# One load tile in four pieces beside the first store, and GpSimdE in charge of the critical section

## Chip, cores and metric

The kernel runs on one core of a Trainium2 chip. The metric is the time of one execution on the device in microseconds. Several chips of the same kind were used. Kernels submitted together ran on one chip, together with new runs of the kernel before, so every comparison has its own yardstick.

## The reference

A softmax over groups of 544 values. The whole tensor is read once and written once, 285 MB each way.

```python
B, N, D, G = 4, 4096, 4352, 8
x_g = x.reshape(B, N, G, D // G)
exp = np.exp(x_g - x_g.max(axis=-1, keepdims=True))
out = (exp / exp.sum(axis=-1, keepdims=True)).reshape(B, N, D)
```

## The kernel before

The 16,384 rows are cut into 64 tiles of 128 partitions with two rows each: 34,816 bytes per partition, 4.456 MB per tile. Six buffers are used in turn. Each tile is loaded, reduced to its maxima (VectorE), exponentiated with sums (ScalarE), multiplied in place by the reciprocal sums (VectorE) and stored. Loads are issued by SyncE, stores by GpSimdE except the last two. The load of tile t waits until the store of tile t-6 has landed on all 16 DMA engines.

```python
ctx.enter_context(tc.tile_critical(no_gpsimd_drain=True))
bufs = [... nc.sbuf_tensor(f"xt{b}", [P, R * D], f32) ... for b in range(NT)]   # NT = 6
...
for t in range(nt):                                   # SyncE: loads, nt = 64
    if t >= NT:
        nc.sync.wait_ge(stored[t % NT], 16 * (t // NT))
    tile_in = bufs[t % NT]
    if t < nt - 1:
        nc.sync.dma_start(out=tile_in[:, :], in_=xt[t]).then_inc(landed[t % NT], 16)
    else:
        ...                                           # the last tile in two halves
for t in range(nt - LAST, nt):                        # SyncE: the last two stores
    nc.sync.wait_ge(scaled, t + 1 if t < nt - 1 else len(parts))
    nc.sync.dma_start(out=ot[t], in_=bufs[t % NT][:, :]).then_inc(last_stored, 16)
nc.sync.wait_ge(last_stored, 16 * LAST)

for t in range(nt - LAST):                            # GpSimdE: the other stores
    nc.gpsimd.wait_ge(scaled, t + 1)
    nc.gpsimd.dma_start(out=ot[t], in_=bufs[t % NT][:, :]).then_inc(stored[t % NT], 16)
...
```

## Time and profile before

| | kernel before |
|---|---|
| time, median of the first 3 runs | 1326.64 us (1326.55 to 1326.76) |
| span in the profile | 1324.9 us |
| rate of the 16 DMA engines, 300 to 1200 us | 433 GB/s |
| time per tile in the middle, load to load | 20.61 us |
| VectorE busy | 1190.0 us, 90% |

The DMA engines are the bound; the prediction shows the lines. In profile lines VectorE is DVE, ScalarE ACT, GpSimdE POOL and SyncE SP; the DMA queue q0 (software_dynamic) carries GpSimdE's stores, q1 (hardware_dynamic) what SyncE issues. Besides the page, the trace holds every DMA packet (queue, size, start, duration) and, for each transfer, 16 landings, one per DMA engine. In a load the distance of the 16th landing from the first tells how far the slowest engine is behind.

### The profile page before, as it was taken

Reading aid. Unit: us, or ns where it says so; the run is one execution under the profiler, and the core shown is the slowest. Engines: PE = TensorE matmul, PEld = TensorE weight load, DVE = VectorE, ACT = ScalarE, POOL = GpSimd, SP = SyncE. Lnnn points to the kernel's source line nnn. Section 1 sums busy time; section 2 is a strip of 40 time slices with the busy share of each in tenths; the row PEclk is TensorE's granted clock in tenths of the full one; section 3 lists DMA queues with packets and bytes.
Section 4 is the critical chain, followed back from the end, with each engine's and each line's share of the span. In section 5 each row is a group of like instructions: output and inputs, shape, how many; then the busy total and the mean of one; then the engine's idle time right before and its main releaser. Section 6 shows DMA issues by size and latency. Waiting matters only on the chain.

```text
span 1324.9 us, 2463 instructions
## 1 busy us (share of the span) xinstructions
DVE 1190.0 (90%) x195; ACT 757.5 (57%) x2049; POOL 33.4 (3%) x66
## 2 busy tenths in 40 slices
DVE  5999999988989889898898998988989889898893
ACT  3765566547456465564655646556465474654751
POOL 0000000000000000000000000000000000000000
DMA  9999999999999999999999999999999999999998
GB/s 404 421 432 436 428 435 434 434 431 433 433 435 433 432 434 433 436 429 435 432 436 431 433 433 434 434 431 435 433 436 429 435 432 436 431 432 434 433 431 372
DMA packets 18582, 570.48 MB, mean 431 GB/s; under 512 B 2064, under 2 KB 2064, under 8 KB 2064
## 3 DMA queue, kind: packets, MB, share of 16 engines
q1 hardware_dynamic: 9648, 294.13, 51.5%
q0 software_dynamic: 8928, 276.30, 48.3%
q14 instruction: 6, 0.05, 0.0%
HBM read 285.21 MB, written 285.21 MB: 431 GB/s over the span
## 4 chain that ended last, share of the span: by engine, by line
another core or an unknown queue 69%; DVE 20%; DMA 7%; ACT 1%; SPq 1%; issue 0%
DVE xt L74 10%; DVE mx L61 10%; DMA out_dram<-xt 4%; DMA xt<-in_x_dram 4%; ACT xt L85 1%; SPq L104 1%; DVE rs L71 0%; SPq L166 0%; SPq L47 0%
## 5 line engine op out<-in xcount | busy, mean ns | idle before, releaser
L85 ACT ACTIVATE xt<-xt,mx 128x544 f32<-128x544 f32 x1024 | 750.2, 734 | 542.7 <-DVE mx L61 542.7
L61 DVE TENSOR_REDUCE mx<-xt 128x16 f32<-128x8704 f32 (+1 forms) x65 | 590.1, 9079 | 111.0 <-DMA xt<-in_x_dram 111.0
L74 DVE TENSOR_TENSOR xt<-xt,rs 128x8704 f32<-128x8704 f32 (+1 forms) x65 | 590.6, 9086 | 2.2
L85 ACT ACTIVATION_READ_ACCUMULATOR xt<-xt,mx 128x1 f32 x1024 | 191.8, 187 | 0.0
L118 POOL DMA_DIRECT2D out_dram<-xt x62 | 33.2, 535 | 1243.7 <-DVE xt L74 1243.7
L71 DVE RECIPROCAL rs<-sm 128x16 f32<-128x16 f32 (+1 forms) x65 | 15.7, 242 | 2.8 <-ACT xt L85 2.8
L123 ACT ACT_TABLE_LOAD x1 | 1.3, 1283 | 0.9 <-SPq L47 0.9
L155 POOL MEMSET const-float32-0.0<- 128x1 f32 x1 | 0.1, 99 | 0.2 <-issue 0.2
L155 POOL MEMSET const-bfloat16-1.0<- 128x1 bf16 x1 | 0.1, 102 | 0.0
L155 POOL MEMSET const-float32-1.0<- 128x1 f32 x1 | 0.1, 99 | 0.0
L155 POOL MEMSET const-uint8-127<- 128x1 uint8 x1 | 0.1, 99 | 0.0
## 6 DMA issues: line engine op xcount, KB each, us to landing
xt<-in_x_dram SPq DMA_DIRECT2D x63, 4352.0 KB, 33.1
out_dram<-xt POOLq DMA_DIRECT2D x62, 4352.0 KB, 50.6
out_dram<-xt SPq DMA_DIRECT2D x2, 4352.0 KB, 20.1
xt<-in_x_dram SPq DMA_DIRECT2D x2, 2176.0 KB, 36.0
```

The source lines that it names most:

```text
L61: i = nc.vector.reduce_max(out=mx[:, t % NT, g], in_=groups(t, g), axis=X, negate=True)
L71: nc.vector.reciprocal(out=rs[:, t % NT, g], in_=sm[:, t % NT, g]).wait_op(exp_done, n + 1, "sem-ge").then_inc(rec_done, 1)
L74: nc.vector.tensor_tensor(out=xg, in0=xg, in1=rs[:, t % NT, g].unsqueeze(2).to_broadcast([P, g.stop - g.start, Dg]), op=mybir.AluOpType.mu ...
L85: i = nc.scalar.activation(out=xg[:, g - gs.start, :], in_=xg[:, g - gs.start, :], func=Exp, bias=mx[:, t % NT, g:g + 1], scale=1.0, accum ...
L104: nc.sync.dma_start(out=tile_in[:, :], in_=xt[t]).then_inc(landed[t % NT], 16)
L118: nc.gpsimd.dma_start(out=ot[t], in_=bufs[t % NT][:, :]).then_inc(stored[t % NT], 16)
L123: nc.scalar.preload_act_table(Exp)
L155: nc = _bacc.Bacc("TRN2", target_bir_lowering=False, num_devices=1)
```

## The change

The intent: when the first store joins the running loads, about one microsecond of DMA time is lost, and the tile then being loaded is tile 4. Its packets are cut to a quarter of their length (8.7 KB). Also, GpSimdE signals the start and the end of the critical section (the `tile_critical` block, in which the kernel orders its engines by its own semaphores) in place of SyncE, to save a hop.

```diff
+    FINE, PIECES = 4, 4
...
-    ctx.enter_context(tc.tile_critical(no_gpsimd_drain=True))
+    ctx.enter_context(tc.tile_critical(
+        sync_engine=mybir.EngineType.Pool, no_gpsimd_drain=True))
...
-            i.wait_op(landed[t % NT], 16 * (t // NT + 1), "sem-ge")
+            more = PIECES - 1 if t % NT == FINE else 0
+            i.wait_op(landed[t % NT], 16 * (t // NT + 1 + more), "sem-ge")
...
-        if t < nt - 1:
+        if t == FINE:
+            for k in range(PIECES):
+                c = slice(k * R * D // PIECES, (k + 1) * R * D // PIECES)
+                nc.sync.dma_start(out=tile_in[:, c], in_=xt[t, :, c]).then_inc(landed[t], 16)
+        elif t < nt - 1:
...
-    nc.sync.wait_ge(last_stored, 16 * LAST)
...
     nc.gpsimd.drain()
+    nc.gpsimd.wait_ge(last_stored, 16 * LAST)
```

## The prediction

> **What bounds the kernel now.** I read the page's slices first, then busy time by stretches, then the DMA view of single stretches, last the instructions at the end. In the slices the 16 DMA engines read 9 or more all the way:
>
> ```profile
> DVE  5999999988989889898898998988989889898893
> DMA  9999999999999999999999999999999999999998
> GB/s 404 421 432 436 428 435 434 434 431 433 433 435 433 432 434 433 436 429 435 432 436 431 433 433 434 434 431 435 433 436 429 435 432 436 431 432 434 433 431 372
> HBM read 285.21 MB, written 285.21 MB: 431 GB/s over the span
> ```
>
> VectorE looks almost as full, but its row dips to 8 in most slices while the DMA row never does. The same in stretches (columns: us, VectorE, ScalarE and GpSimdE busy, clock, DMA share, GB/s):
>
> ```profile
> 0.00:5.00 5.00, 0.00 (x0) 1.28 (x1) 0.20 (x4) 1.00 0.69 223
> 300.00:1200.00 900.00, 811.97 (x131) 518.36 (x1405) 23.45 (x44) 1.00 1.00 433
> 1318.00:1321.00 3.00, 0.00 (x0) 0.00 (x0) 0.00 (x0) 1.00 0.62 267
> 1321.00:1324.90 3.90, 0.00 (x0) 0.00 (x0) 0.00 (x0) 1.00 0.02 9
> ```
>
> So the kernel is bound by 570.4 MB at 433.3 GB/s, 1316.5 us of the 1324.9 us span. I added up the trace's packets in order of time to see where the other 8.4 us go. About 3.0 us are lost in the first 5 us, until loads flow. About 0.9 us are lost between 46 and 51 us and nowhere else in the middle: in single microseconds the rate is 425, 401, 292, 280 and 378 GB/s, then 433 again. The rest is the end: 15 of the 16 engines finish the last store between 1320.3 and 1322.0 us, one at 1323.53 us, and 1.37 us of closing follow. That one engine falls behind all through the run: its part of a load lands 0.24 us after the median part for tile 0, 0.98 us at 308 us, 2.93 us for the last load. It sets the end, so what counts is the time saved on it.
>
> The hole at 46 to 51 us is the one place that the first part of the change touches. The first store is issued at 44.88 us, its first packets start at 49.9 us, and meanwhile load packets that always take 1288 ns are stretched, the longest to 2801 ns. The extra time of those packets sums to 0.90 us per engine. Tile 4 is indeed the tile then in flight: tile 3 lands at 45.2 us and tile 4 at 62.5 us.
>
> **What the Trainium skill says.** The page "DMA: Bandwidth & Descriptors", section "Queues, rings and completion order", says that each DMA engine goes round the queues that have work, one packet each. The trace agrees. With 34.8 KB packets on both sides loads and stores get half each, but in 1263 to 1269 us, where the last tile's loads have 17.4 KB packets, the shares are 2 to 1:
>
> ```profile
> q0 software_dynamic: 51, 1.74, 67.1%
> q1 hardware_dynamic: 49, 0.85, 33.1%
> ```
>
> Almost equal packets (51 and 49), half the bytes: size of packet is weight. The same page, section "Rules for kernel authors", asks for transfers of 1 MiB or more; a piece here is 128 x 8704 B = 1.11 MB, so I charge nothing for the cut. That 17.4 KB packets take 648 ns against 1288 ns for 34.8 KB agrees: no visible cost per packet. "SWDGE vs HWDGE vs iDMA" in that page says that GpSimdE's stores take their descriptors from rings in SBUF; no number in the trace tells whether this makes the hole.
>
> **The change, part by part.**
>
> *Instructions.* Three more load issues on SyncE, about 0.45 us each, at 3 to 5 us, while three tiles (30 us of data) are queued: hidden. VectorE, ScalarE and the stores keep their order. Tile 4's wait is for 64 instead of 16 in its first turn; VectorE wants tile 4 only at 81.6 us, against a landing at 62.5 us, so 19 us of delay are free there.
>
> *The first store starts sooner.* A queue that joins a busy one waits for packets already taken: the store that SyncE issued at 1290.49 us had its first packet at 1294.25 us, about three packets of 1.29 us. With packets a quarter as long (8704 B, estimate 1288/4 = 322 ns) three are 1.0 us. I expect first store packets near 47 us instead of 50. If the stretched packets are a quarter as long, much of the 0.90 us may go. If the stretch is a latency that does not depend on packet size, none does. I take 0.5 us, about half, as a choice.
>
> *Stores get ahead, and loads fall behind.* Beside 8.7 KB loads a store has weight 4 to 1, 347 of 433 GB/s. Store 0 (4.456 MB) takes 12.9 us, from 47 to 59.9 us, instead of 20.6. In the meantime load 4, which had 1.0 MB by 47 us, gets 1.1 MB more. The second store is issued only at 63.43 us and, with about 2 us to its first packet, loads are alone for 5.5 us and get 2.4 MB. So load 4 lands near 65.2 us instead of 62.0 (median engine), 3.2 us late. If the first store comes no sooner than 50 us, the same sum gives 69.0 us, 7 us late. Afterwards both sides alternate evenly and both queues keep work, so every load and all the computing stay late by this amount S, and every store comes as much earlier.
>
> *What S does at the end.* The computing after load 62 is one chain on VectorE without waits for loads:
>
> ```profile
> 1257.81 9.22 DVE L61 TENSOR_REDUCE mx<-xt 128x16 f32<-128x8704 f32 x1 [2.02 <-DMA xt<-in_x_dram]
> 1276.37 4.68 DVE L61 TENSOR_REDUCE mx<-xt 128x8 f32<-128x4352 f32 x1
> 1290.38 4.68 DVE L61 TENSOR_REDUCE mx<-xt 128x8 f32<-128x4352 f32 x1
> 1301.33 4.69 DVE L74 TENSOR_TENSOR xt<-xt,rs 128x4352 f32<-128x4352 f32 x1
> 1306.05 0.34 SPq L112 DMA_DIRECT2D out_dram<-xt  x1
> ```
>
> The last store is issued at 1306.05 us but starts only when store 62 is done, at 1310.5 us on most engines and 1313.3 us on the slow one. With S it can start at 1306.05 + S + about 1 us of issue (the first load's first packet came 1.0 us after its issue), and lasts 10.3 us. On the slow engine S may therefore be 1313.3 - 1307.05 = 6.2 us before it costs anything; 3.2 us are free, 7 us cost 0.8 us. The other engines get a gap of their own that nobody waits for.
>
> *Opening and closing.* SyncE's own signal (0.73 us), its branch (0.80) and its first issue (0.96) are a chain behind GpSimdE's release at 0.62 us. If GpSimdE signals right after its release, I estimate one hop of 0.07 us less. At the end the last store's landing at 1323.53 us is passed on by SyncE, collected by it at 1324.02 us and then handed to GpSimdE's barrier at 1324.17 us; when GpSimdE does both, about 0.08 us of that hop goes. The drain on GpSimdE (5.1 us from 1312.08) ends before the landing and stays off the path. Sum 0.15 us.
>
> *Sum:* 1326.64 - 0.5 (hole) - 0.15 (hops) + 0 (S of 3 us hidden) = 1326.0; for the rivals below I add 0.2 and predict **1326.2 us**.
>
> **The rivals.**
>
> 1. *The hole is only moved, or comes twice.* Store 0 now ends near 60 us and store 1 starts near 65 us, so the switch from loads alone to loads with stores happens twice; before, the first store queue was never empty (store 0 landed at 71.6 us, store 1 was issued at 63.4). For it: the hole came with exactly this switch, and the page shows no other. Against it: SyncE's store joined a running store queue at 1294 us with no hole, so not every new start costs. Two full holes give 1326.64 + 0.9 - 0.15 = 1327.4.
>
> 2. *The first store starts no sooner and S is 7 us.* Then the last store comes too late: 1326.64 + 0.8 - 0.15 = 1327.3; with 2 us from issue to first packet, 1328.3. For it: what is held ahead of a new queue may be bytes and not packets. Against it: the skill's round by packets.
>
> 3. *The hole vanishes wholly:* 1326.64 - 0.9 - 0.15 = 1325.6. For it: someone chose the tile and the piece for this.
>
> 4. *Nothing:* the slow engine, 2.7 us behind at the end, may not share the gain: 1326.5.
>
> **Range and chances.** The main case gives 1325.6 to 1326.4, rivals 1 and 2 put a quarter of the weight at 1327 and above. I take 1325.2 to 1327.6. Two per cent are 26.5 us; the whole loss that any of this touches is under 4 us, so within 2% is nearly certain.
>
> **What would show each step right or wrong.** In the profile after: (a) load 4's packets 512 of 8704 B, 322 ns each; (b) first store packets near 47 us, and the extra time of stretched packets under 0.90 us per engine; (c) while tile 4 loads, stores move about 4 times the bytes of loads, and store 0 lands near 60 us; (d) a stretch near 60 to 65 us with loads alone, with or without a second hole when store 1 starts; (e) load 4, and every later load, about 3 us later, the last store issued about 1309 us; (f) the rate in the middle still 433 GB/s; (g) first load issued near 0.89 us, the closing after the last landing near 1.3 us. The prediction is wrong if the rate in the middle moves, if S exceeds 6 us, or if the holes grow instead of shrinking.

## The result, and the profile after

The changed kernel has no single time. Its first six runs took 1326.48, 1332.17, 1331.41, 1333.08, 1332.55 and 1349.59 us, median 1332.36, against 1326.74 us before (median of six, 1326.55 to 1327.48). Further runs on other chips, listed below, reach 1453.77 us. Ratios in this document are the mean time of one kernel's fast runs over that of the other's of the same rounds, so not quite the ratio of the medians. Here that ratio is 1.0032 (1.0014 to 1.0051), but a run counts as fast if it is at most 1.5% above the fastest of its kernel, and that rule leaves out the slowest run that the change made here, 1349.59 us. The clock reads 1.0 in all of them, and the kernel before, on the same chips and in the same rounds, has only three runs above 1328.1 us, all on one chip, the longest 1333.57. So the slow runs are the result and are kept.

All 22 runs of the changed kernel:

| time | runs |
|---|---|
| 1326.4 to 1326.6 us | 3 |
| 1331 to 1334 us | 8 |
| 1340 to 1376 us | 5 |
| 1406 us | 1 |
| 1450 to 1454 us | 5 |

The first profile fell on a run of the fastest kind, 1326.48 us. Its slices look like those of before:

```profile
DVE  5999999989889898898998988989889898898995
DMA  9999999999999999999999999999999999999998
GB/s 404 419 430 430 436 434 429 433 437 434 429 432 436 436 428 432 437 435 432 430 435 434 433 431 434 435 434 429 433 436 436 427 433 437 435 430 431 435 434 375
```

The DMA view of 52 to 62 us, while tile 4 loads in small packets beside store 0 (per queue: packets, MB, share of the engines' time), shows what the pieces do:

```profile
q0 software_dynamic: 98, 3.38, 78.1%
q1 hardware_dynamic: 102, 0.75, 17.7%
```

Packets are again about equal in number, so the store moves 4.5 times the bytes. Store 0 lands at 62.9 us (median engine) instead of 69.8, loads are then alone until store 1 starts at 66.9 us, and load 4 lands at 66.4 instead of 62.0. At the end everything is 3.5 us later than before, but the last store is still in time:

```profile
1261.33 9.22 DVE L63 TENSOR_REDUCE mx<-xt 128x16 f32<-128x8704 f32 x1 [1.99 <-DMA xt<-in_x_dram]
...
1304.85 4.69 DVE L77 TENSOR_TENSOR xt<-xt,rs 128x4352 f32<-128x4352 f32 x1
...
1309.57 0.34 SPq L119 DMA_DIRECT2D out_dram<-xt  x1
```

The kernel before had 1257.81, 1301.33 and 1306.05 us in these places. Another thing in this trace turned out to be the key. Before, stores ended 7.9 us after loads. Now a load and a store end within 0.2 us of each other (median engine), on every tile of the run. Load 4 ends at 66.4 us and store 1 starts at 66.9 us, so load 5 and store 1 start together, each is eight packets per engine, and nothing parts them again.

The slower runs show up in traces taken later. This is the row for 300 to 1200 us (us; VectorE, ScalarE and GpSimdE busy; clock; DMA share; GB/s), first of the 1326.48 us trace, then of a run of the same kernel that took 1406.02 us:

```profile
300.00:1200.00 900.00, 812.35 (x133) 519.88 (x1408) 23.37 (x44) 1.00 1.00 433
```

```profile
300.00:1200.00 900.00, 770.14 (x126) 489.01 (x1325) 21.78 (x41) 1.00 1.00 411
```

The DMA share reads 1.00 in both. Packets are stretched, and a stretched packet counts as busy. Only the rate tells that something is wrong.

### The profile page after: what moved, and what is told of

It reads as the page before. It is cut to its first block, busy times and chain, and to the rows that moved or that the text cites. A ratio compares the mean times of both kernels' runs of the same rounds, so it can differ in the third digit from the quotient of the medians.

```text
span 1324.7 us, 2468 instructions
## 1 busy us (share of the span) xinstructions
DVE 1190.2 (90%) x195; ACT 757.5 (57%) x2049; POOL 33.3 (3%) x66
## 4 chain that ended last, share of the span: by engine, by line
DMA 70%; DVE 27%; ACT 1%; issue 0%; POOLq 0%; SPq 0%
DMA out_dram<-xt 35%; DMA xt<-in_x_dram 35%; DVE xt L77 14%; DVE mx L63 13%; ACT xt L88 1%; DVE rs L74 0%; SPq L173 0%; POOLq L48 0%; POOLq L162 0%
```

## The experiments

### First call: which part does it

```diff
# e1: the changed kernel again
# e2 fine_only: SyncE opens and closes, as before
-        sync_engine=mybir.EngineType.Pool, no_gpsimd_drain=True))
+        no_gpsimd_drain=True))      # and the wait for last_stored back on SyncE
# e3 pool_only
-    FINE, PIECES = 4, 4
+    FINE, PIECES = 4, 1
# e4 fine_tile2
-    FINE, PIECES = 4, 4
+    FINE, PIECES = 2, 4
```

> The changed kernel once more, for the scatter (1326.5 us in its profiled run, 1331.4 to 1333.1 in four timed ones, 1349.6 in one). Theory A: the slow runs are a second course of the same program, in which the stores get further ahead at the first store (S over 6 us) so that the last store starts late; then some runs give 1326 to 1327 and others 1331 to 1333 on one chip, and the late ones show a gap before the last store. Theory B: the profiled run was on another chip than the timed ones and this chip decides; then all runs of one call agree within 0.5 us.

> The four pieces alone; SyncE opens and closes as before. Theory A (pieces cause the slow runs): scatter as in the changed kernel, about 1332 us in most runs. Rival C (GpSimdE's opening and closing costs it): 1326.2 to 1327 us in all runs.

> GpSimdE opens and closes, tile 4 in one piece. Theory A: 1326.5 us, 0.15 us under the kernel before, no scatter. Rival C: 1332 us in most runs.

> GpSimdE opens and closes; the four pieces are taken by tile 2, whose load is over at 34 us, before the first store. Theory A (what matters is the share of stores and loads while the first store runs): as pool_only, 1326.5 us, no scatter. If small packets cost by themselves: some us more.

Measured, with the kernel before at 1326.52 us (median of 11, 1326.39 to 1328.05):

| run | all times, us |
|---|---|
| e1, changed kernel | 1332.46, 1452.40, 1331.95, 1452.93, 1452.05, 1332.05 |
| e2, pieces alone | 1332.78, 1350.93, 1332.68, 1453.64, 1326.77, 1332.64 |
| e3, GpSimdE alone | 1326.42, 1326.36, 1326.45, 1326.42, 1326.46 |
| e4, pieces in tile 2 | 1327.60, 1327.28, 1327.50, 1327.55, 1327.58 |

The scatter comes with the pieces (e2) and not with GpSimdE (e3), which rules out rival C. It appears within one chip, so theory B falls. Small packets that are over before the first store make no scatter (e4), but 1.0 us of time, where theory A expected none. Its trace shows where it sits: the DMA engine that ends last is already 1.65 us behind the median in the load of tile 4 (0.56 us in the kernel before) and 3.7 us at the end (2.7). Why is not shown.

Theory A, which blamed a late last store, falls too. In the 1332.46 us trace load 4 lands at 66.2 us, no later than in the fast one, but one DMA engine falls behind the others by 0.1 us at each tile, up to 6.6 us at the last load.

To see more, I put the packets of each DMA engine in order. A packet starts 3 ns before the end of the one ahead of it on its engine, so the 16 sequences can mostly be put together from the trace. L is a load packet of 34.8 KB, l one of 8.7 KB, S a store packet. This is around the start of store 1, one engine of each kind:

```
1326.48 us trace, all 16 engines:   l l l l l L S L S L S L S L S L S L S L S | L S L S ...
1332.46 us trace, 3 of 16 engines:  l l l l l L L S L S L S L S L S L S L S S | L L S L ...
```

Store 1 becomes available at about 66.9 to 67.2 us, just while the engines end their first packet of load 5 (66.6 to 67.9 us). An engine that ends it a moment too early takes a second load packet first, and keeps that order for the rest of the run. The chance lies in tenths of a microsecond.

### Second call: traces of the slow runs, other distances

```diff
# e5, e6: the changed kernel, one profiled look each
# e7 pieces2
-    FINE, PIECES = 4, 4
+    FINE, PIECES = 4, 2
# e8 cut45: tile 4 in four pieces and tile 5 in two
-    FINE, PIECES = 4, 4
+    CUT = {4: 4, 5: 2}
...                                 # used in the wait and in the loads
```

> The changed kernel, one look, to see a trace of another of its courses (so far 1326.5, 1332, 1350 and 1452 us). Theory D: since load 4 ends within a packet of the start of store 1, every later load and store begin together on each DMA engine, and the course is set by how many engines start store 1 one load packet late: none in the 1326.5 us trace, three of 16 in the 1332 us trace, where the engine that is last loses 0.12 us at each of the tile ends in one stretched store packet. In a 1350 or 1452 us trace some engines then lose 0.4 or 2 us at each tile end. Theory A (the last store late by a large S): a 1452 us trace would show one large gap and no loss in the middle, which a landing of load 4 below 70 us speaks against already.

> As the look before it, a second try for a trace of another course of the changed kernel; theories D and A expect the same of it as stated there.

> Tile 4 in two pieces of 17.4 KB packets. Stores weigh 2 to 1 while it loads: store 0 ends near 65 us, load 4 near 66.7 us, by when store 1 has some 0.5 MB: loads and stores end about 2 us apart for the rest of the run, over one packet of 1.3 us. Theory D: no engine can start one packet off; 1326 to 1327 us in all runs, no scatter. Rival E (any small packets under the first store cost it): scatter as with four pieces.

> Tile 4 in four pieces as in the change, and tile 5 in two, so that stores get another 2 to 1 lead while tile 5 loads and loads and stores end several us apart afterwards. Theory D: the scatter goes, though tile 4 is cut as in the change; 1326 to 1328 us, somewhat more if the lead makes the last store late. Rival E: scatter as in the change.

Measured: e5 1340.41 us, e6 1406.02 us, e7 1454.33, 1454.50, 1333.21 and 1452.92 us, e8 1328.42, 1334.47, 1329.60 and 1327.37 us. The kernel before on this chip scattered more than elsewhere, 1326.32 to 1333.57 us (seven runs, median 1327.90), so e8, with three of four runs above the 1328 us expected of it, was repeated on another chip (e10).

My expectation for e7 was wrong. Loads and stores did end 2.6 us apart (about 2 was worked out), and that was not far enough: on 15 engines store 1 comes after two load packets, on one after one. That one engine is the slow one. Its store packets, 1288 ns in all good runs, take 1951 to 1971 ns three times running from 75 us on, and again later:

```
e7, 15 engines:   ... L L S L S L S L S      L S      L S      L S S | L L S ...
e7, one engine:   ... L S L S L S+86 L S+681 L S+683  L S+663  L S+67 L S+225 ...   (+ is ns over 1288)
```

It is 3.9 us behind after the first such tile, 8.2 us after the second. By 213 us it is 24 us behind, in the middle of the run 26, which is more than a tile. There it stays, since the load of tile t waits for the store of tile t-6 on *all* engines: the other 15 run out of loads and wait for it. When their loads come again, they suffer the hole of the first store once more (the packets in flight are stretched by about 1.2 us per engine in the tile at 715 us). The time per tile is now that of the slow engine, 22.63 us instead of 20.6; 62 tiles times 2.02 us are 125 us, and the run is 1454 - 1327 = 127 us slow. This one engine accounts for nearly all of it: between 717 and 730 us its store packets alone are stretched by 1.9 us in one tile.

Across the traces with either order on the engines, the time goes with the share of engines with two load packets ahead (us per tile: from the landing of load 12 to that of load 52; stretched: store packets over 1328 ns; lag: last minus first landing of the load of tile 37):

| trace | engines with two loads first | time, us | us per tile | stretched | lag, us |
|---|---|---|---|---|---|
| changed, first profile | 0 | 1326.48 | 20.59 | 20 | 1.0 |
| e1, changed | 3 | 1332.46 | 20.68 | 66 | 3.6 |
| e2, pieces alone | 3 | 1332.78 | 20.68 | 123 | 3.8 |
| e5, changed | 5 | 1340.41 | 20.85 | 1737 | 10.4 |
| e11, changed (below) | 7 | 1367.14 | 21.26 | 2833 | 20.9 |
| e6, changed | 8 | 1406.02 | 21.71 | 2995 | 22.8 |
| e14 (below) | 12 | 1455.20 | 22.63 | 2326 | 26.0 |
| e7, two pieces | 15 | 1454.33 | 22.63 | 1503 | 26.0 |

Which engines pay also changes. Between 72 and 110 us, with at most five engines two loads ahead, no engine's store packets are stretched by more than 0.3 us in sum. With seven or more it is mostly the engines with *one* load first that lose, each 0.6 to 2.0 us with seven, 2.4 to 3.5 us with eight, 4.6 to 6.8 us with twelve and 5.3 us with fifteen.

### Third call: distance or packets

```diff
# e9 late_store1: the kernel before, and
         nc.gpsimd.wait_ge(scaled, t + 1)
+        if t == 1:
+            nc.gpsimd.wait_ge(rec_done, 3)
# e10: as e8; e11: the changed kernel
# e12 after_store1_later: the changed kernel, and
         nc.gpsimd.wait_ge(scaled, t + 1)
+        if t == 1:
+            nc.gpsimd.wait_ge(exp_done, 3)
```

> The kernel before, no small packets; only the second store waits for the third reciprocal (72.4 us), so that it starts near 77 us, about when load 5, by then alone for 7 us, ends. Theory F (what matters is that loads and stores of a tile end within about 3 us of each other on the engines; before, stores end 7.9 us after loads): scatter as in the changed kernel, some runs near 1332 and some over 1340 us. Rival E (the small packets themselves leave the engines in a bad state): 1327 to 1328 us in all runs, the mean loss of a second hole.

> Tile 4 in four pieces and tile 5 in two once more, for more runs beside the changed kernel on one chip: stores end 4.9 us before loads. Theory F: within 1326 to 1330 us, no run over 1340. Rival E: as many slow runs as the changed kernel has.

> The changed kernel beside the others of this call, as their yardstick: on both theories about half of its runs over 1340 us, most others near 1332 us.

> The changed kernel, tile 4 in its four pieces, but the second store waits for the third tile's exponentials (65.4 us instead of 63.2), so that it starts near 69.7 us, 3 us after load 5 has started alone. Stores then end about 6.6 us after loads for the rest of the run, near the 7.9 us of the kernel before. Theory F: 1326 to 1328 us in all runs, no scatter, by a wait of 2 us alone. Rival E: scatter as in the changed kernel.

Measured, with the kernel before at 1326.51 us (median of 11, 1326.42 to 1326.95):

| run | store ends after load by | all times, us |
|---|---|---|
| e9 | -8.4 us | 1328.16, 1327.64, 1327.88, 1329.36, 1327.80 |
| e10 | -4.9 us | 1328.81, 1328.55, 1329.26, 1328.33, 1332.07 |
| e11, changed | 0.2 us | 1367.14, 1332.36, 1326.56, 1368.12, 1375.99, 1450.13, 1453.77, 1326.39 |
| e12 | 6.9 us | 1327.98, 1327.50, 1327.32, 1330.27, 1327.93 |

e12 is the plainest test. It is the changed kernel with its small packets, and the second store is issued 2.7 us later than in the changed kernel's first profile (63.19 us there). This is its GpSimdE timeline:

```profile
65.89 0.53 POOL L126 DMA_DIRECT2D out_dram<-xt  x1 [20.59 <-ACT xt L88]
```

No run is over 1331 us, though one of five, 1330.27 us, is above the 1328 us that I expected at most; the middle runs at full rate:

```profile
300.00:1200.00 900.00, 811.88 (x131) 519.39 (x1408) 23.38 (x44) 1.00 1.00 433
```

In e12 engines also differ, six with three and ten with four load packets ahead of store 1, without harm. So different orders alone do not cost; they do when loads and stores end close together. e9 was a miss as a test: load 7 had to wait for the delayed store 1 (97.2 us), loads ran dry (a second hole, 385 GB/s on average from 100 to 104 us), and the distance became -8.4 us instead of the few I had aimed at. It only adds one more distance without runs over 1330 us. In e10 one run, 1332.07 us, is above the 1330 us that theory F allowed, and none is over 1340 us.

### Fourth and fifth call: in step without small packets, and all engines in one order

```diff
# e13 step_no_pieces: the kernel before, tile 4 whole, and in SyncE's loads
+        if t == 5:
+            nc.sync.wait_ge(scaled, 2)
# e14 delay_a: the changed kernel, and ahead of the second store
+            nc.gpsimd.memset(spare[:, :], 0.0)          # 128x512
# e16 delay_b, e17 delay_c: the same, and then
+            nc.gpsimd.drain()
+            nc.gpsimd.memset(spare[:, :320], 0.0)       # e17: all 512 columns
```

> The kernel before, tile 4 whole; only load 5 waits for the second scaled tile (63.1 us). Store 0 then runs alone from 62 us and ends near 66.3 us, store 1 follows at once, and load 5 joins near 67 us: both run in step from there, without any small packet. Theory F: scatter as in the changed kernel, some runs over 1340 us. Rival E (small packets needed): all runs 1327 to 1329 us.

> The changed kernel with one GpSimdE fill of 128x512 ahead of the second store[...]. Traces so far, by the number of engines that take two load packets before their first of store 1: 0 1326.5, 3 1332.5 and 1332.8, 5 1340, 7 1367, 8 1406, 15 (two pieces) 1454 us. [...]that number should be 8 to 15, and theory F expects most runs at 1400 us and over, none at 1326. If the number does not matter: times as in the changed kernel.

> The changed kernel with two GpSimdE fills (512 and 320 columns) ahead of the second store[...]. Engines with two load packets ahead of store 1: 14 to 16. If 16, all in one order: theory F in the form that a mixed order costs expects 1326 to 1328 us; the form that being in step is enough expects 1450 us. With 14 or 15 both expect 1450.

> As the one before with two fills of 512 columns[...]. All 16 engines with two load packets, or a few with three: in the latter case mixed again, though stores then end 2.8 to 5 us after loads, and the distance counts: 1326 to 1335 us if 5 us are far enough, as they were in the run with tiles 4 and 5 cut.

Measured, with the kernel before at 1326.60 us (e13, e14) and 1326.53 us (e16, e17):

| run | engines with two loads first | all times, us |
|---|---|---|
| e13, no small packet | 13, three with one | 1452.10, 1455.27, 1454.88, 1451.71, 1442.70, 1449.87 |
| e14, store 1 later by 0.2 us | 12, four with one | 1455.20, 1451.97, 1452.28, 1457.53 |
| e16, by 1.0 us | 9, seven with three | 1354.96, 1351.81, 1347.25, 1330.02 |
| e17, by 1.0 us | all 16 | 1344.75, 1349.80, 1350.19, 1345.49 |

(The delays are worked out from the issues of store 0 and store 1: 18.55 us apart in the changed kernel's first profile, 18.77 in e14, 19.52 in e16 and e17. The last two were delayed alike and still differ in the count; for e16 I had expected 14 to 16.) The fill and the issue behind it in e14's GpSimdE timeline:

```profile
63.09 0.52 POOL L126 MEMSET spare<- 128x512 f32 x1 [17.64 <-DVE xt L78]
63.56 0.53 POOL L127 DMA_DIRECT2D out_dram<-xt  x1
```

With 0.2 us of delay all four runs are slow, where most were; with 2.7 us (e12) none is over 1331 us. (The changed kernel itself was not run on the chip of e13 and e14, nor on that of e16 and e17; e11 and e12 shared one.)

e13 settles what the packets have to do with it. It has no small packet. One wait puts load 5 and store 1 in step, and all six runs are 9% slow. Its slices, its row for 300 to 1200 us, and the row of waits that carries the cost (total us, times, longest), first in the kernel before, then in e13:

```profile
DMA  9999999999999999999999999999999999999977
GB/s 401 425 417 416 417 420 403 398 399 388 392 395 397 398 397 392 391 393 395 398 391 397 392 395 397 387 397 397 399 387 390 397 397 398 396 390 397 390 314 301
```

```profile
300.00:1200.00 900.00, 741.21 (x120) 468.05 (x1269) 20.77 (x39) 1.00 0.97 394
```

```profile
DVE mx L61 <- DMA xt<-in_x_dram: 111.0, 51, 14.0
```

```profile
DVE mx L61 <- DMA xt<-in_x_dram: 239.8, 58, 13.9
```

VectorE waits 239.8 us for loads, against 111.0 us in the kernel before; the difference, 129 us, is about the loss (1452.1 - 1326.6 = 125.5 us). The three engines with one load first have their stores stretched by up to 716 ns within the first tile in step; of the 13 others, one does in the next tile.

e17 answers the last question half. With all 16 engines in one order (two loads first, stores ending 2.7 us after loads) no engine falls far behind: the lag at tile 37 is 2.1 us. Yet it takes 1345 to 1350 us, with 983 load packets stretched after 60 us, where the kernel before has none, and the rate from 300 to 1200 us is 426 GB/s:

```profile
300.00:1200.00 900.00, 801.15 (x130) 508.06 (x1376) 22.89 (x43) 1.00 1.00 426
```

One common order at 0.2 us cost nothing (1326.48), at 2.7 us 18 to 24 us, and a mixture of one and two loads first up to 131 us (e14). Both forms of theory F that I had written down for it are wrong in their numbers.

## Why the prediction was wrong

Point by point, by its own steps:

- **The bound** was right for the fast runs: 433 GB/s from 300 to 1200 us, before and after. (The DMA row that I called 9 or more all the way has an 8 in its last slice.)
- **"The first store starts sooner"** failed. First store packets came at 49.4 us, not near 47, and the stretched packets cost 1.22 us per engine in the first profile instead of the 0.4 that I left of 0.90. The first store packet came 4.8 us after the issue, against 5.0 before, so what is held ahead of a joining queue is not three packets of whatever size. My reading of three packets at 1294 us had also counted about 1 us of issue as packets. This term alone has 0.8 us of error; in the 1326.48 us trace it was made up for, since the slowest engine was only 1.9 us behind at the end instead of 2.7. That this run lies 0.3 us from my number is luck; 3 of 22 runs are like it. A growing hole was one of my own signs of being wrong.
- **"Stores get ahead, and loads fall behind"** was right in mechanism and near in size: 4.5 to 1 in bytes, load 4 late by 4.4 us (3.2 worked out for a first store at 47 us, 7 for one at 50 us, which is nearly what came), the last store issued at 1309.57 us (about 1309 worked out), and no cost at the end. The cut was not quite free: 8.7 KB packets took 328 ns, not 322, and ran at about 428 GB/s from 62 to 66 us.
- **The hole coming twice** (rival 1) did not happen: no loss between 62 and 68 us beyond 0.07 us.
- **"Opening and closing"**: the first load went out at 0.90 us instead of 0.96, as said. The closing did not shrink, 1.39 us from landing to end in e3 and in the kernel before, 1.53 us in the changed kernel's first profile. e3's 1326.42 against 1326.52 us agrees with the opening alone, but its ratio, 0.9997 (0.9984 to 1.001), does not part it from nothing.
- **The step that failed and decides the result** is the sentence "Afterwards both sides alternate evenly and both queues keep work, so every load and all the computing stay late by this amount S". I used S only to ask whether the last store comes too late. I did not ask where S puts the ends of the stores against those of the loads: my own numbers, load 4 done at 65.2 us and store 1 starting at 65.4, say that both start together. In the first profile loads 4.4 us later and stores 3.2 us earlier turned the distance of 7.9 us into 0.2. What the runs showed in place of the even alternation: in step, packets are stretched in most runs, one or more engines fall behind, and the middle drops from 433 to as little as 394 GB/s. None of my rivals had this, though a middle rate that moves was among my signs of being wrong.
- **The range** was built on terms of about 1 us each and on the idea that a fixed program has one time. The median of the first six runs, 1332.36 us, was 4.8 us above its upper end, and single runs up to 126 us. Nine of the 22 runs lie outside the 2% that I called nearly certain.

What is shown: the slow runs need loads and stores that end close together, whatever brings them there (e13 without pieces, e12 with them but moved apart). Being close is not enough: 3 of 22 runs of the changed kernel took 1326 us, and in the one with a trace all engines had one order and ended within 0.2 us. What stays open: why the DMA engine stretches packets in that case. The 4-byte completion write that ends each engine's part of a transfer, and comes twice within a packet or two in these runs, is a candidate that no run tests; in the 1326.48 us trace it comes as close on all 16 engines, with only 20 store packets stretched, so it can't be the whole cause. Nor do the runs say exactly how far apart is enough: stores 4.9 us ahead of loads (e10, at most 5.6 us slow) or 6.9 us behind (e12, at most 3.8) were far enough, 2.7 us was not, and e16, with engines near 2.7 and others near 5.3 us, was slow in three of four runs.

Neither the changed kernel nor any of the variants beats the kernel before by more than the noise; e3, the second part of the change alone, costs nothing that these runs can show and gains nothing that they can show.

## What to carry to other kernels

Where loads and stores of equal size share the DMA engines, look at when each ends: a one-time nudge at the start (a packet size, a wait of 2 us) sets their distance for the whole run, and in step it cost up to about 10% (e13, e14), with the DMA share still reading 0.97 to 1.00. Run a change several times, on more than one chip, before trusting one profile: the first one here showed 1326.48 us, the next five runs 1331 to 1350. And when the time scatters with one kernel and not with its neighbour in the same rounds, the slow runs are a finding, not a disturbance to be dropped.

## What the Trainium skill lacked or had wrong

- Page "DMA: Bandwidth & Descriptors", section "Queues, rings and completion order": the round of one packet each holds here (51 to 49 and 98 to 102 packets, bytes in the ratio of packet sizes). It does not say that two queues whose transfers end close together can slow each other: 433 to 394 GB/s, packets of 1288 ns stretched to 1950 ns and more. No page has it.
- No page has the loss when a store first joins running loads: 0.7 to 1.0 us per engine with 34.8 KB load packets (0.90 in the kernel before), 1.0 to 1.2 us with 8.7 KB packets.
- Same page, section "Rules for kernel authors": it says that transfers of different queues share the engines and interleave. It gives no size for what it costs when one of the 16 engines falls behind the rest: 26 us behind, 127 us in e7.
- Same page, section "Latency and other measured facts", tells of two engines that are usually slower than the rest, without saying by how much. These traces do not number the engines, but one of the 16 falls behind steadily even in the kernel before, from 1.0 us at 308 us to 2.9 us at the last load.
